# The scheduler counts a port of SBUF that VectorE and GpSimd take by turns; an expert's token rows are gathered two experts ahead

## The chip, the cores and the metric

The program runs on one core of a Trainium2 chip. What counts is the device time of one execution in microseconds (us), as the median of several runs. Five engines work side by side, each through its own queue in order: TensorE (PE, matmuls, with PEld for its weight loads), VectorE (DVE), ScalarE (ACT), GpSimd (POOL) and SyncE (SP, which here only issues DMAs and loads registers). An instruction waits on semaphores for others, and everything behind it in the same queue waits with it.

## What is computed

One encoder layer for 2048 tokens of width 1024: differential attention (4 heads with two score matrices each) beside gated linear attention (GLA), cross-attention to 256 memory tokens, and a mixture of 32 experts, of which each token takes two. The last part in the reference:

```python
def expert_block(args):
    xb, e = args
    hid = jax.nn.silu(xb @ w_gate[e]) * (xb @ w_up[e])
    return hid @ w_down[e]
```

and the differential attention, whose combination of two softmaxes is the place that most of the text below is about:

```python
p = probs(qb1, k1) - lam * probs(qb2, k2)
return jnp.einsum('bhqk,bhkv->bhqv', p.astype(v.dtype), v)
```

Matmuls run in float16 with each operand split into a high and a low half, three products for one. So every tensor that goes into a matmul is first split: ACT writes the high half, and DVE or POOL subtracts it from the float32 value to get the low half.

## The kernel before

Four stages follow each other. **Stage A1** (0 to about 625 us) projects the tokens and runs the GLA heads. **Stage A2** (to about 1155 us) is the differential attention, by blocks of 128 queries and 4 heads. **Stage C** (to about 1600 us) is the cross-attention and the routing of tokens to experts. **The MoE stage** runs the experts, two fixed ones first, then 30 that `rank` orders by their number of tokens.

In A2 each head goes twice (s = 0, 1) through a loop: `scores` has PE write up to four PSUM banks `sc` of 512 keys, DVE takes the minimum of each bank (`mx<-sc`) and of the four (`m<-mx`), ACT takes the exponential (`e<-sc,m`), which frees the banks for the next scores. Once both halves of a head are there, `combine` has DVE form `e1 + cc * e2` in float32 (`e<-e,cc`, a scalar_tensor_tensor with both operands in SBUF, in chunks of up to 1024 keys), ACT cast it (`e<-e`), POOL subtract the cast (`e<-e` on POOL), and SP transpose it by DMA (`pT<-e`) for PE's `po<-VC,pT`. `queries` has DVE copy and POOL subtract on a tile `qc`, `da_norm` and `out_proj` have DVE subtract on `mcd` and `hc`.

In the MoE stage `split_expert` loads an expert's weights in 12 DMAs of 0.5 MB (`est`, 8 buffers of tag E), which ACT and DVE split into `ew` (28 buffers of tag W, shared with the transposed tokens `exT`). `tokens` loads a list of row numbers (`lt<-lists`, issued by SP, with the expert's number read into a register by a TENSOR_LOAD of `order`), gathers the rows with an indirect DMA issued by POOL (`ex<-xnS,lt`, 4 buffers of tag Q), and has PE transpose them (`pxT`) and ACT and DVE copy them to `exT`. `expert` runs the matmuls `pgu` and `py`, and POOL issues the scatter-add `out_dram<-ey,lt`, which still reads `lt`, so a buffer of `lt` (6 of them) is free only after the scatter of its chunk. Each list, gather and scatter is for a chunk of up to 128 rows; most experts have two chunks.

The order on each engine is not written by hand. All operations are recorded, and `flush` runs a list scheduler over them: `price` gives each a cost in ns, `pick` takes for each engine the operation that could start first (ties within 1 ns go to the lower `prio`, which is the place in the program plus a shift by group and engine from the table `SHIFT`), and buffers are given out in the order of the program within a tag. A register load is priced at 100 ns. Before the change `pick` takes DVE and POOL as independent of each other:

```python
t = max(f, o.ready, lane[e][-8] + 110 if o.dma else 0)
```

The emitted order is fixed; on the chip only the waits move.

Of the kernel before, what the change touches and what calls it, by code (L numbers as in the profile page):

```python
# [8 lines left out]
F16 = mybir.dt.float16  # L9
# [29 lines left out]
THR = 0  # L39
# [15 lines left out]
        124, 122, 118, 118, 116, 114, 112, 112, 106, 104, 160, 176, 32]  # L55


TAGS = {"W": (4096, 28), "E": (4096, 8), "P": (4096, 3), "X": (4096, 4), "Q": (4096, 4), "t2": (2048, 4), "t1": (1024, 2), "r": (160, 5), "lt": (32, 6),
        "s8": (32, 5), "sq": (32, 6), "mx": (32, 8), "cb": (32, 6), "so": (32, 6), "c8": (32, 5), "c9": (32, 6), "q8": (32, 4), "grT": (512, 1)}
BANKS = {"mm": 3, "av": 1, "sc": 4}  # L60
AP = bass.AP
# [33 lines left out]

class Op:
    __slots__ = ("i", "eng", "method", "args", "kw", "cost", "need", "users", "ready", "prio", "opens", "tiles", "dma",
                 "start", "end", "fn", "group", "chain")


class Program:
# [4 lines left out]
    def __init__(self, nc, tc):  # L106
        self.nc, self.tc = nc, tc
        for e in ("tensor", "vector", "scalar", "gpsimd", "sync"):
            setattr(self, e, Engine(self, e))
        self.ops, self.tags, self.bufs = [], {}, {}  # L110
        self.log = {}
        self.shift, self.group = 0, ""
        self.chain = None
        self.free = {e: 0 for e in ("tensor", "vector", "scalar", "gpsimd", "sync")}
        self.dma_free = self.hw_free = 0
# [46 lines left out]
    def record(self, eng, method, a, k, fn=None):  # L162
# [48 lines left out]
        o.need = list(need)  # L211
        self.ops.append(o)
        return o

    @staticmethod
    def size(ap):
# [44 lines left out]
    def flush(self):  # L261
# [61 lines left out]
        while len(order) < n:  # L323
# [13 lines left out]
            if o.dma:  # L337
                if e == "gpsimd":
                    self.free[e] = t + 1040
                    s = t + 1770  # L340
                else:
                    self.free[e] = t + 60
                    h = max(self.hw_free, t + 120)
                    turn = "transpose" in o.method
                    s = max(self.dma_free, h + (1275 if turn else 1100))
                    self.hw_free = max(h + 1175, s + o.cost - 927) if turn else h + 475
                s = max(self.dma_free, s)
                self.dma_free = s + o.cost
# [39 lines left out]
class Layer:  # L388
# [1042 lines left out]
    def begin_moe(self):  # L1431

        nc = self.nc
        self.ident16 = self.gate_b[:, 128:192].bitcast(F16)
        nc.vector.tensor_copy(self.ident16, self.ident)
        which, need, self.first = self.expert_weights(None, 0)
        self.prog.shift = EARLY
        cap = CAPS[NE - FIXED]
        tokens = self.tokens(cap, which, need, blocks=LATE)
        self.second = self.expert_weights(None, 1, [self.last] if THR else [], CHAIN)  # L1440
        self.expert(cap, self.first, tokens)
        self.prog.shift = 0

    def stage_moe(self):
# [4 lines left out]
        ready = {}  # L1449

        def prepare(n):
            s = slots[n]
            if n == 0:
                which, need, w = lambda: NE, (), self.first
            elif n < FIXED:
                which, need, w = self.second
            else:
                if n == FIXED:
                    self.rank()
                which, need, w = self.expert_weights(s, None)  # L1460
            self.prog.shift = FRONT
            ready[n] = w, self.tokens(CAPS[s], which, need)
# [9 lines left out]
    def expert_weights(self, rank, e, after=(), chain=0):  # L1472

        nc, a, prog = self.nc, self.a, self.prog
        reg = []
        need = []
        if e is None:
            need = [prog.call("sync", lambda nc: reg.append(nc.sync.value_load(
                self.order[0:1, rank:rank + 1], min_val=0, max_val=NE - 1)), [], [self.order], method="value_load")]
        which = (lambda: reg[0]) if e is None else (lambda: e)  # L1480
        return which, need, self.split_expert(which, need + list(after), STAG if e == 0 else "E", chain)

    def split_expert(self, which, need, tag="E", chain=0):
        self.prog.group = "ew"
# [22 lines left out]
    def tokens(self, cap, which, need, first=None, blocks=0):  # L1507

        self.prog.group = "tk"
        nc, prog = self.nc, self.prog  # L1510
        xT = [self.tile("W", "exT", [8, cap], F16) for _ in range(2)]
        rest = []
        for t0 in range(0, cap, 128):
            n = min(128, cap - t0)
            lt = self.tile("lt", "lt", [2], I32)
# [2 lines left out]

            g = -(-n // 16) * 16
            m = g if parts == 1 else 128 // parts  # L1520
            rest.append((t0, m, lt, parts))

            def load(nc, lt=lt, m=m, t0=t0, parts=parts):
                e = which()
                if first is not None:
# [5 lines left out]
                if parts > 1:  # L1531
# [5 lines left out]
                out=x[:g].rearrange("p t d -> p (t d)"), out_offset=None, in_=self.xnS[:S + OFF - blocks * 128],  # L1537
                in_offset=bass.IndirectOffsetOnAxis(ap=lt[:g, 0:1], axis=0)), [x[:g]],
                      [lt[:g], self.xnS[:S + OFF - blocks * 128]])
            for h in range(2):  # L1540
                p = self.prog.tile(self.ps, [128, 8, 128], F16, "pxT", "mm", BANKS["mm"])
                for k in range(8):
# [65 lines left out]
    def stage_over(self):  # L1608
# [5 lines left out]
        with self.tc.For_i(0, total, 1):  # L1614
# [21 lines left out]
            self.expert(128, w, self.tokens(128, which, (), lambda: row))  # L1636


# [24 lines left out]
```

## Time and profile before

| | |
|---|---|
| median of 3 runs | 2382.82 us (2374.73 to 2393.74) |
| the profiled execution | 2377.83 us, span 2376.1 us |
| PE busy | 2137.9 us (90% of the span) |
| DVE busy | 1559.7 us (66%) |
| ACT busy | 1339.2 us (56%) |
| POOL busy | 750.6 us (32%) |
| mean DMA rate | 204 GB/s |

The profile is one execution, recorded by the hardware. Busy time is the time in which an engine had an instruction running; a wait is idle time of an engine, put down to what ended it. An instruction that the engine has started but that is held inside counts as busy, and shows only as a duration above that of its like. Rows of the profile name operations by the tiles they write and read, as `out<-in`.

### The profile page before, as it was taken

To read this page: it belongs to the slowest core of one execution; us is meant where nothing else is said; L and a number is where in the kernel's file an instruction comes from. 1 tells how busy PE (TensorE), PEld (TensorE's weight loads), DVE (VectorE), ACT (ScalarE), POOL (GpSimd) and SP (SyncE) were. 2 spreads that over 40 slices of the span, in tenths; PEclk is the share of its full clock that TensorE was granted. 3 is DMA by queue.
4 is the path that set the end of the run, shared out by engine and by line. 5 is a ranking of instruction groups with operands and counts; after the bars stand their busy time and mean duration, and the time that the engine had idled before them with its cause. 6 is when DMAs were issued, how large, how long until landed. Compare 5 with 4: busy or idle time off the path is not lost. (4 is left out here: it accounts for less than half of the span.)

```text
span 2376.1 us, 55935 instructions
## 1 busy us (share of the span) xinstructions
PE 2137.9 (90%) x22153; PEld 1466.6 (62%) x22153; DVE 1559.7 (66%) x3434; ACT 1339.2 (56%) x2848; POOL 750.6 (32%) x622
## 2 busy tenths in 40 slices
PE   6999999999888889889998999994899999888888
PEld 3456646556444445445665777843777887777666
DVE  7454445655588888888534655476666877777774
ACT  6455345554466666665433333444566777667775
POOL 1444235552134444444221222213132322222111
PEclk9999999999989999999999999997899999999999
DMA  9544246663357686888785556495989999999995
GB/s 258 155 114 116 81 142 178 192 191 103 111 116 149 145 179 151 184 169 201 168 211 131 116 143 126 117 250 140 300 303 329 345 369 331 325 338 340 358 346 152
DMA packets 504232, 485.34 MB, mean 204 GB/s; under 512 B 391364, under 2 KB 401886, under 8 KB 503966
## 3 DMA queue, kind: packets, MB, share of 16 engines
q1 hardware_dynamic: 489950, 442.11, 64.9%
q0 software_dynamic: 14016, 39.63, 7.2%
q8 instruction: 175, 2.87, 0.5%
q14 instruction: 91, 0.75, 0.1%
HBM read 306.28 MB, written 83.61 MB: 164 GB/s over the span
## 5 line engine op out<-in xcount | busy, mean ns | idle before, releaser
L166 DVE SCALAR_TENSOR_TENSOR ew<-est,ew 128x1024 f16<-128x1024 f32 x384 | 459.8, 1220 | 95.1 <-ACT ew L166 91.5
L166 PE MATMUL pgu<-exT,ew 128*128 128x160 f16 (+27 forms) x6336 | 451.5, 227 | 4.8 <-issue 2.3
L166 PEld LDWEIGHTS <-ew 128*128 128x128 f16 x6336 | 409.7, 100 | 13.6 <-issue 7.5
L166 ACT ACTIVATE ew<-est 128x1024 f16<-128x1024 f32 x384 | 392.8, 1051 | 33.7 <-DMA est<-in_w_e_down_dram 23.9
L166 PEld LDWEIGHTS <-uT 128*128 128x128 f16 x1920 | 187.7, 98 | 224.1 <-issue 9.7
L166 PE MATMUL py<-ew,hid 128*128 128x512 f16 (+4 forms) x1584 | 244.8, 348 | 8.2 <-DVE hid L166 6.2
L166 PE MATMUL sc<-KC,qT 128*128 128x512 f16 (+3 forms) x640 | 171.0, 359 | 57.9 <-ACT e L166 53.9
L166 ACT ACTIVATE e<-sc,m 128x512 f32<-128x512 f32 (+3 forms) x288 | 179.2, 631 | 75.6 <-DVE m L166 49.0
L166 POOL TENSOR_TENSOR e<-e 128x1024 f16<-128x1024 f32 (+7 forms) x96 | 152.3, 1591 | 215.5 <-ACT e L166 165.7
L166 DVE TENSOR_REDUCE mx<-sc 128x1 f32<-128x512 f32 (+3 forms) x320 | 185.4, 603 | 51.1 <-PE sc L166 50.8
L166 PE MATMUL ph<-wo,mT 128*128 128x512 f16 x768 | 194.2, 380 | 8.2 <-DMA mT<-mcd 3.9
L166 PE MATMUL pc<-hT,wcq 128*128 128x128 f16 x3072 | 193.8, 220 | 1.6 <-DMA hT<-hcS 1.0
L166 PEld LDWEIGHTS <-wcq 128*128 128x128 f16 x3072 | 181.6, 98 | 4.9 <-DMA hT<-hcS 1.5
L166 PE MATMUL phc<-wco,prT 128*128 128x512 f16 x768 | 175.9, 382 | 4.3 <-DMA prT<-prc 4.3
L166 PEld LDWEIGHTS <-hid 128*128 128x128 f16 (+4 forms) x1584 | 106.0, 104 | 108.9 <-issue 19.9
L1603 POOL DMA_INDIRECT out_dram<-ey,lt x33 | 65.0, 1969 | 263.9 <-ACT ey L166 218.2
L166 PEld LDWEIGHTS <-qT 128*128 128x128 f16 x640 | 60.0, 99 | 118.4 <-issue 75.8
L166 PE MATMUL po<-VC,pT 128*128 128x128 f16 x1632 | 123.1, 221 | 6.2 <-DMA pT<-e 4.9
L166 PEld LDWEIGHTS <-prT 128*128 128x128 f16 x768 | 74.2, 98 | 87.0 <-DMA prT<-prc 4.4
L166 PEld LDWEIGHTS <-mT 128*128 128x128 f16 x768 | 72.6, 98 | 83.2 <-DMA mT<-mcd 5.8
L166 PEld LDWEIGHTS <-pT 128*128 128x128 f16 x1632 | 103.6, 99 | 29.2 <-DMA pT<-e 9.7
L166 ACT CAST e<-e 128x1024 f16<-128x1024 f32 (+7 forms) x96 | 76.5, 798 | 69.1 <-DVE e L166 36.0
(320 smaller groups left out, 3700.1 us busy)
## 6 DMA issues: line engine op xcount, KB each, us to landing
est<-in_w_e_gate_dram SPq DMA_DIRECT2D x128, 512.0 KB
est<-in_w_e_up_dram SPq DMA_DIRECT2D x128, 512.0 KB
est<-in_w_e_down_dram SPq DMA_DIRECT2D x128, 512.0 KB
wst<-in_w_in_dram SPq DMA_DIRECT2D x20, 512.0 KB
xt<-in_x_dram SPq DMA_DIRECT2D x16, 512.0 KB
uS<-uT SPq DMA_DIRECT2D x16, 512.0 KB
ust<-in_w_ckv_dram SPq DMA_DIRECT2D x16, 512.0 KB
uT<-uS SPq DMA_DIRECT2D x16, 512.0 KB
```

The lines of the kernel that those rows point to most:

```text
L166: o.fn = fn or (lambda nc: getattr(getattr(nc, eng), method)(*a, **k))
L1603: self.prog.call("gpsimd", lambda nc: nc.gpsimd.indirect_dma_start(out=out, out_offset=bass.IndirectOffsetOnAxis(ap=rows, axis=0), in_=y, ...
```

## The change

`shares_port` marks the operations that use a port taken by turns: on GpSimd tensor_tensor and tensor_scalar with more than 8 columns, on VectorE two-input operations with both large operands in SBUF, and copies and tensor_scalar from SBUF to SBUF. In `flush` there is one more time, `port_free`: a marked operation can't start before it, on either engine, and sets it to its end. Costs, shifts and the operations themselves stay as they were, but the order on every engine is made anew with this rule.

In the MoE stage `tokens` is cut in two: `fetch` (the list and the gather) and `turn` (transposes and copies). `stage_moe` calls `fetch` for expert n+2 ahead of `turn` for expert n+1, and `lt` has 12 buffers instead of 6. `expert_weights` is cut likewise; the register load moves to `chosen`, which `fetch` calls.

```diff
-"t1": (1024, 2), "r": (160, 5), "lt": (32, 6),
+"t1": (1024, 2), "r": (160, 5), "lt": (32, 12),
...
+        o.port = self.shares_port(eng, method, outs, ins)
...
+    def shares_port(self, eng, method, outs, ins):
+
+        if eng == "gpsimd":
+            return method in ("tensor_tensor", "tensor_scalar") and self.size(outs[0]) > 8
+        n = sum(x.space != PSUM for x in ins)
+        if method in ("tensor_tensor", "scalar_tensor_tensor"):
+            return eng == "vector" and sum(x.space != PSUM for x in ins if self.size(x) > 1 or self.size(outs[0]) == 1) > 1
+        return eng == "vector" and method in ("tensor_copy", "tensor_scalar") and n > 0 and outs[0].space != PSUM
...
-                t = max(f, o.ready, lane[e][-8] + 110 if o.dma else 0)
+                t = max(f, o.ready, lane[e][-8] + 110 if o.dma else 0, self.port_free if o.port else 0)
...
                 self.free[e] = o.end = t + o.cost
+                if o.port:
+                    self.port_free = o.end
+                    dirty.update(("vector", "gpsimd"))
...
+        def prepare(n):
+            which, need, got = rows.pop(n)
+            w = self.first if n == 0 else self.second[2] if n < FIXED else self.split_expert(which, need)
+            self.prog.shift = FRONT
+            ready[n] = w, self.turn(CAPS[slots[n]], got)
+            self.prog.shift = 0
+        fetch(0)
+        fetch(1)
         prepare(0)
         for n, s in enumerate(slots):
+            if n + 2 < len(slots):
+                fetch(n + 2)
             if n + 1 < len(slots):
                 prepare(n + 1)
```

The first place is on DVE in stage A2, for one head of a block with 1792 keys: `mx` and `m1` are the minima that the loop waits for, `e_1367` and `e_1368` the two chunks of the head before. One piece of the difference:

```order
 L166 SCALAR_TENSOR_TENSOR cc_1406<-rs_1250,s2_1405,nlam_1019 128x1
-L166 SCALAR_TENSOR_TENSOR e_1367<-e_1379,cc_1406,e_1367 128x1024
 L166 TENSOR_REDUCE mx_1409<-sc_1410 128x1
 L166 TENSOR_REDUCE mx_1409<-sc_1411 128x1
 L166 TENSOR_REDUCE mx_1409<-sc_1412 128x1
 L166 TENSOR_REDUCE mx_1409<-sc_1413 128x1
+L166 TENSOR_SCALAR r1t_1285<-sst_1284 128x1
+L166 SCALAR_TENSOR_TENSOR e_1367<-e_1379,cc_1406,e_1367 128x1024
+L166 TENSOR_REDUCE m1_1414<-mx_1409 128x1
+L166 COPY r1_1143<-r1r_1286 128x1
 L166 SCALAR_TENSOR_TENSOR e_1368<-e_1380,cc_1406,e_1368 128x768
-L166 TENSOR_REDUCE m1_1414<-mx_1409 128x1
```

The first chunk moved behind the four minima, and both chunks now stand close together, with `m1` between them instead of behind the second.

The second place is on SP, where `rank` has just ordered the experts: `lt` are the lists of rows, TENSOR_LOAD reads an expert's number, `est` are the weights of the first ranked expert. The order before:

```order
L1533 DMA lt_3345<-lists_1034 128x1x2
L1478 TENSOR_LOAD order_3366
...
L1533 DMA lt_3401<-lists_1034 128x2
...
L1499 DMA est_3375<-in_w_e_gate_dram 128x1024
...
L1499 DMA est_3387<-in_w_e_up_dram 128x1024
L1478 TENSOR_LOAD order_3366
...
L1499 DMA est_3389<-in_w_e_up_dram 128x1024
```

The same place in the changed kernel:

```order
L1500 TENSOR_LOAD order_3348
...
L1556 DMA lt_3357<-lists_1034 128x2
...
L1556 DMA lt_3359<-lists_1034 96x2
...
L1556 DMA lt_3428<-lists_1034 128x2
...
L1525 DMA est_3383<-in_w_e_gate_dram 128x1024
...
L1525 DMA est_3387<-in_w_e_gate_dram 128x1024
L1500 TENSOR_LOAD order_3348
...
L1556 DMA lt_3475<-lists_1034 128x2
...
L1525 DMA est_3389<-in_w_e_gate_dram 128x1024
```

Before, one list and seven weight loads follow the first three register loads, and 20 register loads come ahead of the eighth weight load. Now five lists and three weight loads follow, and 26 register loads and two more lists come ahead of the fourth weight load.

The third place is on POOL a little later: `ex` with 96 rows is the second chunk of the second fixed expert, which PE waits for, and `ey` are the scatters of the experts ahead of it. The order before:

```order
L1536 DMA ex_3402<-xnS_1033,lt_3401 128x2048
L1603 DMA out_0_dram<-ey_3299,lt_3258 2176x1024
L1603 DMA out_0_dram<-ey_3302,dst_3304 8704x256
L1603 DMA out_0_dram<-ey_3358,dst_3360 8704x256
L1536 DMA ex_3406<-xnS_1033,lt_3405 96x2048
```

And in the changed kernel:

```order
L1559 DMA ex_3358<-xnS_1033,lt_3357 128x2048
L1637 DMA out_0_dram<-ey_3299,lt_3256 2176x1024
L1559 DMA ex_3360<-xnS_1033,lt_3359 96x2048
L1637 DMA out_0_dram<-ey_3302,dst_3304 8704x256
L1559 DMA ex_3380<-xnS_1033,lt_3379 128x2048
```

The gather of the 96 rows passed two scatters. Stage C keeps its order on every engine.

## Rows read from the trace of the kernel before

**Rows 1.** Windows by stage: length; busy PE, PEld, DVE, ACT, POOL; clock; DMA; GB/s

```profile
0.00:625.00 625.00, 578.48 (x5064) 350.80 (x5066) 326.98 (x757) 319.62 (x775) 244.51 (x181) 0.99 0.53 151
625.00:1155.00 530.00, 454.10 (x3355) 253.13 (x3352) 442.01 (x943) 335.73 (x856) 218.57 (x148) 0.97 0.74 159
1155.00:1600.00 445.00, 429.93 (x4910) 313.88 (x4909) 240.70 (x872) 163.75 (x426) 96.79 (x147) 0.99 0.64 156
...
1660.00:1760.00 100.00, 90.89 (x1118) 73.88 (x1117) 61.12 (x103) 60.53 (x93) 22.35 (x16) 0.90 0.91 293
1760.00:2340.00 580.00, 530.80 (x7068) 432.85 (x7067) 439.87 (x601) 423.06 (x636) 143.01 (x82) 0.96 1.01 342
```

**Rows 2.** Waits of 625 to 1155 us: who <- for whom: us in total, times, longest

```profile
ACT e L166 <- DVE m L166: 79.7, 48, 4.2
PE sc L166 <- ACT e L166: 53.9, 40, 5.6
DVE mx L166 <- PE sc L166: 50.8, 38, 4.5
```

**Rows 3.** Groups by form, DVE, 625 to 1155 us: count | busy us, mean ns | idle

```profile
L166 DVE SCALAR_TENSOR_TENSOR e<-e,cc 128x1024 f32<-128x1024 f32 x40 | 56.0, 1399 | 1.2
...
L166 DVE COPY qc<-qc 128x512 f16<-128x512 f16 x30 | 18.4, 618 | 1.9 <-POOL qc L166 1.0 <-ACT qc L166 0.7
...
L166 DVE SCALAR_TENSOR_TENSOR e<-e,cc 128x896 f32<-128x896 f32 x8 | 11.9, 1493 | 0.1
L166 DVE SCALAR_TENSOR_TENSOR e<-e,cc 128x768 f32<-128x768 f32 x8 | 11.9, 1491 | 0.2
L166 DVE SCALAR_TENSOR_TENSOR e<-e,cc 128x640 f32<-128x640 f32 x8 | 10.7, 1332 | 0.0
...
L166 DVE SCALAR_TENSOR_TENSOR e<-e,cc 128x384 f32<-128x384 f32 x8 | 8.2, 1024 | 0.1
L166 DVE SCALAR_TENSOR_TENSOR e<-e,cc 128x512 f32<-128x512 f32 x8 | 8.0, 1002 | 0.1
```

**Rows 4.** The same view for POOL, 625 to 1155 us

```profile
L166 POOL TENSOR_TENSOR e<-e 128x1024 f16<-128x1024 f32 x40 | 87.0, 2175 | 131.1 <-ACT e L166 109.9 <-issue 21.3
```

**Rows 5.** Timeline, 807 to 830 us: start, length, instruction [idle before, releaser]

```profile
807.10 1.01 POOL L166 TENSOR_TENSOR ror<-rot,mhalf 128x4 f32<-128x4 f32 x1 [3.15 <-DVE s L166]
807.64 1.28 DVE L166 SCALAR_TENSOR_TENSOR e<-e,cc 128x1024 f32<-128x1024 f32 x1
...
813.31 0.87 DVE L166 SCALAR_TENSOR_TENSOR e<-e,cc 128x640 f32<-128x640 f32 x1
...
823.63 1.28 DVE L166 TENSOR_REDUCE mx<-sc 128x1 f32<-128x512 f32 x2
...
824.72 2.13 POOL L166 TENSOR_TENSOR e<-e 128x1024 f16<-128x1024 f32 x1 [1.16 <-ACT e L166]
824.83 2.70 DVE L166 SCALAR_TENSOR_TENSOR e<-e,cc 128x640 f32<-128x640 f32 x1
...
828.25 0.28 DVE L166 COPY qc<-qc 128x512 f16<-128x512 f16 x1
828.45 0.14 DVE L166 TENSOR_REDUCE m<-mx 128x1 f32<-128x4 f32 x1
...
829.46 0.59 PE L166 MATMUL sc<-KC,qT 128*128 128x512 f16 x2 [1.71 <-ACT e L166]
```

**Rows 6.** MoE: register loads on SP, count: ns min/median/max, first and last start

```profile
L1478 SPq TENSOR_LOAD <-order x30: 261/268/815, 1655.0 to 1677.8; - x30
```

**Rows 7.** MoE, timeline of SP and of PE: lists, and a wait for gathered rows

```profile
1680.38 1.62 SPq L1533 DMA_DIRECT2D lt<-lists  x2
...
1694.05 0.82 PE L166 MATMUL pxT<-gb,ex 96*128 96x96 f16 x8 [4.78 <-DMA ex<-xnS,lt]
```

**Rows 8.** MoE, who waited for tile ex, and SP's waits: us, times, longest

```profile
  PE pxT L166: 20.7, 7
...
SPq L1533 <- DMA out_dram<-ey,lt: 35.4, 13, 6.0
```

More of the change, by code (lines that the diff above doesn't have):

```diff
@@ L55 @@
         124, 122, 118, 118, 116, 114, 112, 112, 106, 104, 160, 176, 32]
-TAGS = {"W": (4096, 28), "E": (4096, 8), "P": (4096, 3), "X": (4096, 4), "Q": (4096, 4), "t2": (2048, 4), "t1": (1024, 2), "r": (160, 5), "lt": (32, 6),
+TAGS = {"W": (4096, 28), "E": (4096, 8), "P": (4096, 3), "X": (4096, 4), "Q": (4096, 4), "t2": (2048, 4), "t1": (1024, 2), "r": (160, 5), "lt": (32, 12),
         "s8": (32, 5), "sq": (32, 6), "mx": (32, 8), "cb": (32, 6), "so": (32, 6), "c8": (32, 5), "c9": (32, 6), "q8": (32, 4), "grT": (512, 1)}
@@ L97 @@
     __slots__ = ("i", "eng", "method", "args", "kw", "cost", "need", "users", "ready", "prio", "opens", "tiles", "dma",
-                 "start", "end", "fn", "group", "chain")
+                 "start", "end", "fn", "group", "chain", "port")
 class Program:
@@ L114, in __init__ @@
         self.free = {e: 0 for e in ("tensor", "vector", "scalar", "gpsimd", "sync")}
-        self.dma_free = self.hw_free = 0
+        self.dma_free = self.hw_free = self.port_free = 0
     def tile(self, pool, shape, dtype, name, tag, bufs):
@@ L1435, in begin_moe @@
         nc.vector.tensor_copy(self.ident16, self.ident)
-        which, need, self.first = self.expert_weights(None, 0)
+        which, need, self.first = self.expert_weights(0)
         self.prog.shift = EARLY
         cap = CAPS[NE - FIXED]
-        tokens = self.tokens(cap, which, need, blocks=LATE)
-        self.second = self.expert_weights(None, 1, [self.last] if THR else [], CHAIN)
+        tokens = self.turn(cap, self.fetch(cap, which, need, blocks=LATE))
+        self.second = self.expert_weights(1, [self.last] if THR else [], CHAIN)
         self.expert(cap, self.first, tokens)
@@ L1448, in stage_moe, with fetch @@
         slots += [k + j * n for k in range(n) for j in range(3)]
-        ready = {}
-        def prepare(n):
+        ready, rows = {}, {}
+        def fetch(n):
             s = slots[n]
             if n == 0:
-                which, need, w = lambda: NE, (), self.first
+                which, need = lambda: NE, ()
             elif n < FIXED:
-                which, need, w = self.second
+                which, need, _ = self.second
             else:
@@ L1459, in prepare @@
                     self.rank()
-                which, need, w = self.expert_weights(s, None)
+                which, need = self.chosen(s)
             self.prog.shift = FRONT
-            ready[n] = w, self.tokens(CAPS[s], which, need)
+            rows[n] = which, need, self.fetch(CAPS[s], which, need)
             self.prog.shift = 0
+        def prepare(n):
[6 more added lines that the diff above has]
+        fetch(1)
         prepare(0)
         for n, s in enumerate(slots):
+            if n + 2 < len(slots):
+                fetch(n + 2)
             if n + 1 < len(slots):
@@ L1470, in stage_moe, with chosen, expert_weights @@
             self.prog.shift = 0
-    def expert_weights(self, rank, e, after=(), chain=0):
-        nc, a, prog = self.nc, self.a, self.prog
+    def chosen(self, rank):
         reg = []
[L1476 to L1481, printed above, removed]
+        need = [self.prog.call("sync", lambda nc: reg.append(nc.sync.value_load(
+            self.order[0:1, rank:rank + 1], min_val=0, max_val=NE - 1)), [], [self.order], method="value_load")]
+        return (lambda: reg[0]), need
+    def expert_weights(self, e, after=(), chain=0):
+        which = lambda: e
+        return which, [], self.split_expert(which, list(after), STAG if e == 0 else "E", chain)
     def split_expert(self, which, need, tag="E", chain=0):
@@ L1505, in split_expert, with fetch @@
         return get("w_e_gate", D, DE, 2), get("w_e_up", D, DE, 2), get("w_e_down", DE, D, 1)
-    def tokens(self, cap, which, need, first=None, blocks=0):
+    def fetch(self, cap, which, need, first=None, blocks=0):
         self.prog.group = "tk"
         nc, prog = self.nc, self.prog
-        xT = [self.tile("W", "exT", [8, cap], F16) for _ in range(2)]
-        rest = []
+        rows = []
         for t0 in range(0, cap, 128):
@@ L1520, in tokens @@
             m = g if parts == 1 else 128 // parts
-            rest.append((t0, m, lt, parts))
             def load(nc, lt=lt, m=m, t0=t0, parts=parts):
@@ L1539, in tokens, with turn @@
                       [lt[:g], self.xnS[:S + OFF - blocks * 128]])
+            rows.append((t0, n, x, m, lt, parts))
+        return rows
+    def turn(self, cap, rows):
+        self.prog.group = "tk"
+        nc = self.nc
+        xT = [self.tile("W", "exT", [8, cap], F16) for _ in range(2)]
+        rest = []
+        for t0, n, x, m, lt, parts in rows:
+            rest.append((t0, m, lt, parts))
             for h in range(2):
@@ L1635, in stage_over @@
             w = self.split_expert(which, ())
-            self.expert(128, w, self.tokens(128, which, (), lambda: row))
+            self.expert(128, w, self.turn(128, self.fetch(128, which, (), lambda: row)))
 def kernel(**inputs):
```

## The prediction

> **What bounds the kernel now.** I read the windows by stage first, because the change touches two stages in different ways. In A1 PE is busy for 578 of 625 us, in stage C for 430 of 445 us [rows 1]: both are PE's own work, and little can be won there by moving DVE or POOL. In A2 PE is busy for 454 of 530 us and DVE for 442 of 530 us, so neither is full and about 76 us of PE's time are idle. In the MoE stage from 1760 us the DMA engines are full (share 1.01, 342 GB/s) and PE is busy for 531 of 580 us: two limits lie close together there. Only in the 100 us after `rank` does DMA have some room (0.91, 293 GB/s) [rows 1].
>
> Then I read the waits in A2, to see what its idle 76 us are made of. They form one loop: PE waits for ACT's exponential (53.9 us in 40 waits), ACT waits for the minimum `m` (79.7 us in 48 waits), and DVE's `mx` waits for PE's scores (50.8 us) [rows 2]. Whatever delays `m` goes once around the loop and ends as idle PE. What delays `m` is not a wait that a view of waits could name. The timeline shows it as a duration: DVE needed 2.70 us for an `e` of 640 keys that took 0.87 us elsewhere, while POOL ran its own `e` of 1024 keys from 824.72 us for 2.13 us. `m` followed at 828.45 us, and PE's next scores at 829.46 us, after 1.71 us of idleness [rows 5].
>
> **Term 1, the combination in A2.** How much of DVE's time is such holding follows from the means by form. Clean prices from the timeline are 1.28 us for 1024 keys and 0.87 us for 640 [rows 5], so 0.41 us for 384 keys more; by that slope an `e` of 896, 768, 512 or 384 keys costs 1.14, 1.01, 0.73 or 0.60 us clean (estimates). Against the means [rows 3] the excess is 40 x 0.12 = 4.8 us for 1024 keys, then 8 x 0.35 = 2.8, 8 x 0.48 = 3.9, 8 x 0.46 = 3.7, 8 x 0.27 = 2.2 and 8 x 0.43 = 3.4 us for the shorter ones: 20.8 us together. The copies `qc` have a mean of 618 ns [rows 3] and took 0.28 us when POOL was idle [rows 5]: 30 x 0.34 = 10.1 us. Together DVE is held for about 31 us. That the shorter chunks suffer most fits the order: they stand directly behind the first chunk, when POOL works on what ACT has cast of it, and POOL takes 2.18 us for one of these [rows 4], 87.0 us in all.
>
> With the change the scheduler no longer plans a DVE `e` inside a POOL `e`. The order shows how it gets there: both chunks stand next to each other, ahead of POOL's work on the first, and the minima pass them. This removes no work; it only turns holding into useful order. Upper bound of the gain: all 31 us, which PE's 53.9 us of waiting for ACT [rows 2] could contain. Lower bound: 0, if the held instructions were those that nothing waited for, or if POOL is late instead and its `e` delays the transposes. On one hand the one example that I followed passed fully to PE (1.71 us of a holding of 2.70 - 0.87 = 1.83 us [rows 5]). On the other hand DVE is idle for 530 - 442 = 88 us in A2 [rows 1] and absorbs some holdings, and the planned times of the other engines are not those of the chip, so some collisions will come back at other places. I take half: **-15 us**.
>
> A row and a rule differ here. POOL's `ror` (4 columns) ran for 1.01 us from 807.10 us, and DVE's `e` that started inside it took 1.28 us, its clean time [rows 5]; so leaving ops of up to 8 columns unmarked costs nothing by the trace. The Trainium skill, page "SBUF — State Buffer", section "Who interferes with whom", says that whoever issues first gets the shared pair of ports for the whole instruction, and that the issue order, not the shape, decides who blocks. The long collisions agree with it; by its letter that `e` would have ended some 0.47 us later than it did, the small ops would go on holding DVE, and the gain would be nearer 10 than 15 us. The measurement decides, and the sum goes by the row.
>
> **Term 2, A1.** The same rule reorders pieces of A1, but PE has 578 of 625 us there [rows 1], and what is idle is spread over many short gaps. Bounds: a few us either way. I take 0; the work that hides it is PE's own, and if PE were late in the gated attention the cost would show as PE waits on DVE or POOL in A1.
>
> **Term 3, the gathers.** In the MoE stage PE waited 20.7 us in 7 waits for gathered rows [rows 8], once 4.78 us at 1694 us [rows 7], in the stretch in which DMA had room. SP waited 35.4 us in 13 waits for the scatter to free a list buffer [rows 8]; behind it in SP's queue stand the weight loads, which is why this can matter to PE too. Fetching two experts ahead with 12 list buffers should end most of both. But from 1760 us DMA is full [rows 1]; what PE doesn't wait for rows it will wait for weights, and SP's waits there cost nothing while enough loads are outstanding. So the bounds are 0 and -20.7 us (the SP waits lie within these, or are hidden by full queues), and I take the part in the stretch with room and a little more: -7 us.
>
> Against it stands what the change puts ahead of the first ranked expert's weights. Five lists stand before the first weight load instead of one: 4 more at 0.81 us (1.62 us for two [rows 7]) are 3.2 us. And 26 register loads with two more lists now come ahead of the fourth weight load, where before 20 came ahead of the eighth. 26 x 0.268 us [rows 6] and two lists are 8.6 us at least; by the pace of the 30 before, 22.8 us for all [rows 6], up to 20 us. Four weight loads of 0.5 MB, issued later than they were, are 2 MB, at 342 GB/s [rows 1] about 6 us of DMA work that isn't done in the meantime. Bounds 0 (the two fixed experts' matmuls cover it, and the weights are needed only behind these) and +9 us. I take +3, so term 3 is **-4 us**. The register loads lie in the same stretch as the wait of 4.78 us, so gain and loss will be seen side by side.
>
> **Sum.** -15 + 0 - 4 = -19 us. The profiled execution took 2377.83 us, so it would take about 2359; it lies 5 us below the median of the runs, 2382.82, from which the forecast is 2382.8 - 19 = **2364 us**.
>
> **Rivals.**
> *The holding only moves (nothing changes).* The plan's times are sums of priced costs, on the chip the engines drift by more than the 0.87 to 2.70 us that matter here, and POOL's `e` has 87.0 us [rows 4] that must lie somewhere beside DVE's 442 [rows 1]. For it: DVE and POOL are marked together for most of a block. Against it: the two chunks are now neighbours by order, which no drift undoes. The time would be 2382.8 - 4 = 2379 us.
> *More is won.* All 31 us of holding and most of PE's 20.7 us for rows go: 2382.8 - 31 - 17 = 2335 us. For it: the followed example passed on 94% of its holding. Against: full DMA in the MoE stage, idle DVE in A2.
> *Slower: the combination comes too late.* The `e` now stand behind four minima, 4 x 0.64 us = 2.6 us later [rows 5], and these minima themselves wait for PE's scores. Behind `e` stand ACT's cast, POOL's subtraction and the transposes, for which PE's `po` waits. Each of the 80 chunks of [rows 3] that makes PE wait that long costs 2.6 us; from one in seven on (11 x 2.6 = 29 us) it takes more than term 1 gives, and at one in five (16, so 42 us) the time is 2382.8 - 19 + 42 = 2406 us. For it: PE has no more than 76 us of room in A2 [rows 1]. Against: PE has the scores of the next heads to do meanwhile.
>
> **How the numbers follow.** The forecast has a chance of 0.48, and its own range is 2345 to 2380 us; the holding that only moves 0.22; more won 0.12; slower 0.18. The range has to leave out no more than 2 in 10: half of the large gain (0.06) falls below 2335 us, and most of the slower case (0.13) beyond 2400 us. 1% is about 24 us, and about what a measurement of this kernel can tell from no change, since its own runs spread from 2374.73 to 2393.74 us. Faster by over 1% (below 2359) are the large gain and some two fifths of the forecast, 0.12 + 0.20 = 0.32. Slower by over 1% (above 2407) is most of the slow case, 0.15. Within 1% is the rest, 0.53.
>
> **What the changed profile would show.** Right: the means of `e` on DVE fall towards 1.28 us (1024) and 0.87 us (640), `qc` towards 0.28 us; PE's wait for ACT's `e` in A2 falls from 53.9 us by about 15, and A2 becomes as much shorter; PE no longer waits for `ex`, SP's lists no longer wait for scatters. Wrong: these means fall and A2 keeps its length (then the held instructions were not on the path); POOL's `e` grows beyond 2.18 us by as much as DVE gains (the holding moved); PE waits for `pT` in A2 (the slower rival); or PE waits for the first ranked expert's weights around 1700 us for more than the 4.78 us that go (then the register loads cost what the gathers gave).

## The result and the profile after

The changed kernel took **2355.93 us** (median of 4 runs, 2353.85 to 2358.44), the kernel before 2380.76 us beside it (4 runs); the ratio is 0.989, with a 95% interval of 0.985 to 0.993. That is 25 us less, where 19 were forecast. The profiled execution of the changed kernel has a span of 2356.6 us (before 2376.1).

The sum is near, but its parts are not. To see that, one must not look at the stages by fixed times, since they shift, but ask when the same instruction starts in both traces:

| us from the start | before | after | moved |
|---|---|---|---|
| first `pq` (end of A1) | 578.2 | 577.9 | -0.3 |
| first `pc` (first matmul of stage C) | 1162.7 | 1146.6 | -16.0 |
| first `phc` (first output projection of stage C) | 1225.3 | 1225.1 | -0.1 |
| first `pgu` (first expert) | 1634.0 | 1637.6 | +3.6 |
| end of the last `py` | 2364.8 | 2345.5 | -19.3 |

A2 is 16 us shorter, all of that is gone 79 us later, and the time that is left at the end comes from the MoE stage alone: 730.8 us from the first `pgu` to the last `py` before, 707.9 us after.

The windows of the changed kernel, columns as in [rows 1]:

```profile
0.00:625.00 625.00, 581.66 (x5067) 353.13 (x5068) 331.17 (x758) 319.47 (x777) 239.72 (x181) 0.99 0.54 151
625.00:1155.00 530.00, 469.73 (x3509) 268.88 (x3509) 427.27 (x958) 338.18 (x861) 222.31 (x151) 0.95 0.75 166
1155.00:1600.00 445.00, 418.63 (x4712) 303.83 (x4710) 231.19 (x839) 158.15 (x415) 92.90 (x142) 0.98 0.59 145
...
1660.00:1760.00 100.00, 83.99 (x1064) 67.55 (x1065) 59.09 (x108) 54.40 (x87) 27.84 (x19) 0.90 0.91 299
1760.00:2340.00 580.00, 548.27 (x7432) 446.98 (x7430) 455.51 (x624) 438.62 (x663) 126.59 (x82) 0.97 0.99 342
```

In A2 PE did 154 matmuls more in the same 530 us, while DVE's busy time fell by 15 us. In the last window PE got through 364 matmuls more. (The last row's DMA rate still reads 342 GB/s, because its final weights landed before 2340 us here; a window that ends earlier is shown below.)

The waits of the same stretch of A2, in answer to [rows 2]:

```profile
DVE mx L166 <- PE sc L166: 55.1, 60, 3.0
ACT e L166 <- DVE m L166: 46.9, 34, 6.4
...
PE sc L166 <- ACT e L166: 26.6, 16, 2.6
```

PE's wait for the exponential fell from 53.9 to 26.6 us, ACT's wait for `m` from 79.7 to 46.9 us. And DVE by form, in answer to [rows 3]:

```profile
L166 DVE SCALAR_TENSOR_TENSOR e<-e,cc 128x1024 f32<-128x1024 f32 x40 | 51.5, 1287 | 0.8
L166 DVE COPY qc<-qc 128x512 f16<-128x512 f16 x30 | 17.4, 580 | 7.6 <-ACT qc L166 5.4 <-POOL qc L166 2.1
L166 DVE SCALAR_TENSOR_TENSOR e<-e,cc 128x896 f32<-128x896 f32 x8 | 11.0, 1374 | 0.1
L166 DVE SCALAR_TENSOR_TENSOR e<-e,cc 128x768 f32<-128x768 f32 x8 | 9.3, 1166 | 0.0
L166 DVE SCALAR_TENSOR_TENSOR e<-e,cc 128x640 f32<-128x640 f32 x8 | 7.9, 991 | 0.0
L166 DVE SCALAR_TENSOR_TENSOR e<-e,cc 128x512 f32<-128x512 f32 x8 | 5.9, 744 | 0.0
L166 DVE SCALAR_TENSOR_TENSOR e<-e,cc 128x384 f32<-128x384 f32 x8 | 5.9, 731 | 0.1
```

The 1024-key `e` is down to its clean price (1287 ns). The shorter forms are not, and `qc` is far from the 280 ns that the prediction hoped for: the copies hardly changed (618 to 580 ns). All six forms of `e` together lost 106.7 - 91.5 = 15.2 us, against 20.8 us that stood above the clean prices.

**Where the 16 us of A2 went.** The trace before and the trace after, cut at the first `pc` and the first `phc`:

```profile
0.00:1162.70 1162.70, 1039.27 (x8450) 607.07 (x8451) 772.57 (x1711) 657.18 (x1635) 464.65 (x331) 0.98 0.63 155
1162.70:1225.30 62.60, 62.34 (x802) 50.88 (x803) 24.38 (x71) 21.76 (x61) 10.45 (x17) 1.00 0.83 212
```

```profile
0.00:1146.60 1146.60, 1043.04 (x8425) 613.65 (x8425) 753.60 (x1702) 655.95 (x1634) 459.74 (x329) 0.97 0.63 157
1146.60:1225.10 78.50, 69.78 (x825) 55.28 (x826) 28.12 (x83) 22.22 (x61) 12.37 (x19) 0.93 0.67 173
...
1180.00:1190.00 10.00, 6.33 (x41) 3.59 (x40) 3.14 (x9) 1.72 (x4) 0.77 (x2) 0.98 0.47 120
1190.00:1200.00 10.00, 5.17 (x51) 4.68 (x51) 4.88 (x16) 5.00 (x14) 3.25 (x5) 0.50 0.49 131
```

Between the two marks PE had almost no idle time before (busy 62.34 of 62.60 us), but 8.7 us after; in the window from 1190 to 1200 us, in which it stood until 1192.47 us and then ran again, its granted clock was 0.50, that is, the lower of its two levels, 1.2 GHz. And 24 matmuls `ph` that were done ahead of the first `pc` now stand behind it (109 instead of 85, 25.9 us instead of 20.2). So of the 16 us about 6 were never won, only put off, and about 10 were won and lost again. PE's timeline shows where, after:

```profile
1192.47 0.35 PE L166 MATMUL pss<-ones,s2c 128*128 128x1 f16 x8 [6.14 <-DVE mf L166]
...
1193.13 1.12 PE L166 MATMUL po<-VC,pT 128*128 128x128 f16 x9 [0.31 <-DVE rct L166]
...
1195.99 0.50 PE L166 MATMUL po<-VC,pT 128*128 128x128 f16 x3 [1.74 <-DMA pT<-e]
1196.80 11.91 PE L166 MATMUL pc<-hT,wcq 128*128 128x128 f16 x184 [0.30 <-ACT ec L166]
```

And before:

```profile
1184.11 7.08 PE L166 MATMUL pc<-hT,wcq 128*128 128x128 f16 x124 [0.17 <-ACT e L166]
...
1191.03 0.34 PE L166 MATMUL pss<-ones,s2c 128*128 128x1 f16 x8
1191.23 3.51 PE L166 MATMUL pc<-hT,wcq 128*128 128x128 f16 x60
```

`pss` (the sums of squares that norm the cross-attention's queries) needs the one bank of PSUM (the memory that PE's matmuls write to) that `po` of the last blocks uses, and that is free only once DVE has formed `mf` from it. Before, 124 matmuls `pc` cover that time. After, nothing does: the whole of that `pc` (184 matmuls) stands behind `pss`. The chain of waits of the changed kernel runs through just this place:

```profile
1185.99 0.35 PE po L166 x6
...
1186.36 0.42 ACT sqo L166
...
1186.86 1.24 ACT hc L166 x3
...
1188.12 0.69 DVE hc L166
...
1190.40 1.03 POOL ror L166
```

From `po` the chain goes by a square on ACT, with ACT's and DVE's `hc` of another block in its way, and POOL's `ror` to `mf`: 6 us in which PE stood.

### The profile page after: what moved, and what is told of

It reads as the page before. It is cut to its first block, busy times and chain, and to the rows that moved or that the text cites. A ratio compares the mean times of both kernels' runs of the same rounds, so it can differ in the third digit from the quotient of the medians.

```text
span 2356.6 us, 55878 instructions
## 1 busy us (share of the span) xinstructions
PE 2141.2 (91%) x22153; PEld 1469.0 (62%) x22153; DVE 1545.7 (66%) x3434; ACT 1338.3 (57%) x2848; POOL 729.8 (31%) x622
## 4 chain that ended last, share of the span: by engine, by line
PE 38%; DMA 8%; DVE 4%; issue 4%; ACT 3%; POOL 2%; SPq 2%; another core or an unknown queue 0%; POOLq 0%; ACTq 0%; DVEq 0%
PE pgu L166 13%; PE py L166 8%; PE pc L166 5%; PE phc L166 4%; PE ph L166 2%; PE pcs L166 2%; ACT ew L166 1%; PE pxT L166 1%; DMA lists<-row,dest 1%; DMA est<-in_w_e_down_dram 1%; PE pq L166 1%; DMA xTr<-xc 1%; DVE ew L166 1%; DMA mT<-gS 1%; PE sc L166 1%
## 5 line engine op out<-in xcount | busy, mean ns | idle before, releaser
L166 PEld LDWEIGHTS <-ew 128*128 128x128 f16 x6336 | 404.7, 98 | 17.6 <-issue 11.6
L166 ACT ACTIVATE ew<-est 128x1024 f16<-128x1024 f32 x384 | 394.3, 1050 | 25.6 <-DMA est<-in_w_e_down_dram 14.9
L166 PE MATMUL ph<-wo,mT 128*128 128x512 f16 x768 | 199.0, 387 | 11.0 <-DMA mT<-gS 8.3
L166 PE MATMUL sc<-KC,qT 128*128 128x512 f16 (+3 forms) x640 | 172.2, 364 | 30.0 <-ACT e L166 26.6
L166 PE MATMUL po<-VC,pT 128*128 128x128 f16 x1632 | 133.7, 226 | 13.7 <-DMA pT<-e 10.0
L166 PEld LDWEIGHTS <-pT 128*128 128x128 f16 x1632 | 110.1, 102 | 39.5 <-DMA pT<-e 14.8
L1637 POOL DMA_INDIRECT out_dram<-ey,lt x33 | 56.6, 1714 | 237.1 <-ACT ey L166 211.9
L1559 POOL DMA_INDIRECT ex<-xnS,lt x52 | 65.0, 1250 | 173.2 <-PE pxT L166 144.9
L166 POOL TENSOR_TENSOR uhl<-ust,uhl 128x1024 f16<-128x1024 f32 x44 | 95.0, 2165 | 58.3 <-ACT uhl L166 54.2
```

The lines of the kernel that those rows point to most:

```text
L166: o.fn = fn or (lambda nc: getattr(getattr(nc, eng), method)(*a, **k))
L1559: prog.call("gpsimd", lambda nc, x=x, lt=lt, g=g: nc.gpsimd.indirect_dma_start(out=x[:g].rearrange("p t d -> p (t d)"), out_offset=None, i ...
L1637: self.prog.call("gpsimd", lambda nc: nc.gpsimd.indirect_dma_start(out=out, out_offset=bass.IndirectOffsetOnAxis(ap=rows, axis=0), in_=y, ...
```

## The experiments

Each run has its kernel before beside it on the same chip (2381.2 us for e1 to e4 and e9 to e11, 2386.3 us for e5 to e8); ratios are to that.

| run | what it is | median us | ratio [95%] | first `pc` | first `phc` | first `pgu` to last `py` |
|---|---|---|---|---|---|---|
| before | | 2380.8 | 1 | 1162.7 | 1225.3 | 730.8 |
| after | | 2355.9 | 0.989 [0.985, 0.993] | 1146.6 | 1225.1 | 707.9 |
| e1 | scheduler's rule alone | 2375.0 | 0.998 [0.995, 1.001] | 1143.0 | 1221.6 | 729.9 |
| e2 | fetch ahead, 12 lists | 2350.4 | 0.987 [0.983, 0.992] | 1157.6 | 1220.1 | 706.3 |
| e3 | 12 lists alone | 2358.5 | 0.990 [0.985, 0.994] | 1163.3 | 1225.9 | 710.7 |
| e4 | fetch ahead, 6 lists | 2378.1 | 0.999 [0.996, 1.001] | 1159.8 | 1222.4 | 728.1 |
| e5 | after, other order of `ph` | 2343.1 | 0.982 [0.978, 0.986] | 1147.6 | 1210.5 | 701.4 |
| e6 | after, rule for `e` alone | 2336.1 | 0.980 [0.976, 0.984] | 1141.5 | 1212.2 | 698.7 |
| e7 | before, POOL only writes `e` | 2353.0 | 0.984 [0.979, 0.990] | 1132.2 | 1194.6 | 741.4 |
| e8 | 8 lists alone | 2351.5 | 0.986 [0.982, 0.989] | 1162.5 | 1225.1 | 702.0 |
| e9 | before, e5's order of `ph` | 2395.0 | 1.006 [1.004, 1.008] | 1176.6 | 1239.4 | 732.1 |
| e10 | e6, other order of `ph` | 2333.6 | 0.981 [0.979, 0.983] | 1141.8 | 1204.2 | 706.2 |
| e11 | e10 with one ahead, 8 lists | 2327.0 | 0.979 [0.977, 0.981] | 1137.5 | 1199.9 | 701.8 |

The last three columns are read from one profiled execution each. Kernels with the same order up to stage C (before, e2, e3, e4, e8) differ by up to 6 us in the first `pc`, so a few microseconds there mean nothing. The distance from the first `pc` to the first `phc` is steadier: 62.4 to 62.9 us in ten of the traces, 78.5 and 78.6 us in the changed kernel and e1, 70.7 us in e6.

**e1 to e4: which half of the change, and which part of that half.** e1 is the kernel before with `shares_port` and `port_free` added. e2 is the changed kernel without them:

```diff
-        o.port = self.shares_port(eng, method, outs, ins)
+        o.port = False
```

> The kernel before with the scheduler's new rule alone; lists and gathers as before. Theory A (read off the two traces: in the changed kernel stage C's first matmuls began 16 us earlier, but its first output projection began at the same time as before, 1225 us): A2 is shorter by 15 to 20 us, all of it is lost again before 1230 us, and the total stays within 5 us of the kernel before, about 2381 us. Rival B (the prediction's sum): the A2 gain stays to the end, total 2366 us, 15 us less.

Theory A held: first `pc` 20 us earlier, first `phc` 4 us earlier, and 6 us less at the end (5 were allowed for), by a ratio that can't be told from no change (0.995 to 1.001). In e1 PE stands at the same `pss` for the same 6.14 us.

> The changed kernel without the scheduler's rule: lists and gathers two experts ahead, 12 list buffers. Theory A (the MoE stage of the changed trace was 23 us shorter): about 2358 us, with the whole gain behind 1650 us and PE waiting no more for gathered rows. Rival B (the prediction's sum): 4 us less than before, 2377 us.

2350.4 us, 8 us below theory A's 2358: the whole gain of the change, and rather more, comes with the fetch and its lists alone. PE has no wait for gathered rows left in this trace. The prediction's -4 us is out.

> The kernel before with 12 list buffers instead of 6 and nothing else; rows are fetched one expert ahead. Theory A1 (the gain in the MoE stage is SP's: it no longer stands still for scatters, 17 us in waits of over 0.5 us in the trace before): 15 to 20 us less than before, about 2363 us, with PE's waits for gathered rows mostly gone. Theory A2 (the gain is that rows come an expert earlier): within 4 us of before, about 2380 us, and PE still waits some 20 us for rows.

The edit of e3, a piece of one line:

```diff
-"r": (160, 5), "lt": (32, 6),
+"r": (160, 5), "lt": (32, 12),
```

> The fetch two experts ahead without the scheduler's rule and with the 6 list buffers of before, so the complement of the run with 12 lists alone. Theory A1: no gain, 2376 to 2385 us, since a list's buffer still comes free only with a scatter. Theory A2: 15 to 23 us less than before, about 2360 us.

These two are the clearest pair: one number alone gives 0.990, and all the rewriting of `tokens` without that number 0.999. (e3's 2358.5 us are some 5 us below theory A1's 2363.) In the traces, PE's waits for `ex` are gone with 12 lists, and 17.7 us in 6 waits with 6 lists (20.7 us in 7 before, [rows 8]). The stretch in which weights stream shows the same split. Before:

```profile
1760.00:2300.00 540.00, 495.99 (x6640) 405.35 (x6639) 409.86 (x563) 394.18 (x595) 139.71 (x80) 0.96 1.01 342
```

After:

```profile
1760.00:2300.00 540.00, 508.27 (x6816) 413.06 (x6814) 429.56 (x584) 413.45 (x620) 120.49 (x79) 0.97 1.02 354
```

e3 (12 lists alone), and e4 (fetch ahead with 6 lists):

```profile
1760.00:2300.00 540.00, 509.46 (x6802) 414.42 (x6800) 427.68 (x583) 411.43 (x618) 121.61 (x78) 0.97 1.02 354
```

```profile
1760.00:2300.00 540.00, 497.38 (x6654) 405.67 (x6653) 413.00 (x567) 397.34 (x599) 134.56 (x81) 0.97 1.01 342
```

So 342 GB/s was not the most that the DMA engines could do. With the waits for rows gone they moved 354 GB/s, 3.5% more; over 540 us that is 19 us of weights.

How one number does that is seen at one of the seven waits of the kernel before, at 1835 us:

```profile
1822.22 2.35 POOL L1603 DMA_INDIRECT out_dram<-ey,dst  x1 [9.64 <-ACT hid L166]
1824.87 1.91 POOL L1536 DMA_INDIRECT ex<-xnS,lt  x1 [0.30 <-issue]
1827.09 1.06 POOL L1536 DMA_INDIRECT ex<-xnS,lt  x1 [0.30 <-issue]
```

```profile
1835.62 0.54 PE L166 MATMUL pxT<-gb,ex 54*128 54x54 f16 x8 [4.56 <-DMA ex<-xnS,lt]
```

```profile
1830.00:1835.00 5.00, 1.06 (x20) 0.88 (x16) 4.22 (x5) 2.61 (x4) 2.00 (x1) 0.85 1.04 271
1835.00:1840.00 5.00, 4.38 (x47) 4.31 (x48) 0.00 (x0) 1.06 (x1) 0.00 (x0) 0.50 1.05 345
```

PE waits for the first of the two gathers: the DMA whose landing ends PE's wait was issued at 1824.87 us, right behind a scatter for which POOL had stood 9.64 us, and landed at 1835.58 us. With six lists the scheduler can place this gather no earlier, since a list comes free only with a scatter. PE stands for 4.56 us, then runs at the lower clock (0.50). As long as it stands it uses up no weights, so their buffers don't come free either: from 1830 to 1835 us the DMA engines moved 271 GB/s, though their share read 1.04. In e3, with 12 lists, the gather of the same rows stands ahead of that scatter and of two others:

```profile
1791.82 2.67 POOL L1536 DMA_INDIRECT ex<-xnS,lt  x1 [8.38 <-PE pxT L166]
1794.79 1.60 POOL L1603 DMA_INDIRECT out_dram<-ey,lt  x1 [0.30 <-issue]
```

PE uses these rows at 1837.32 us there, without a wait; in e8 below the gather went out at 1773.77 us and PE used the rows at 1821.15 us.

SP's own waits were not the cost. SP waited 35.4 us for scatters before [rows 8], 14.9 us after, 23.4 us in e3, and 41.3 us in e8 below, which is among the fastest. My theory A1 gave SP's stalls as the mechanism; the size came out near, but the mechanism is the place of the gather.

**e8: how many lists.** The edit, a piece of the same line:

```diff
-"r": (160, 5), "lt": (32, 6),
+"r": (160, 5), "lt": (32, 8),
```

> The kernel before with 8 list buffers (6 before, 12 in the change); rows one expert ahead. Theory A (what was short is room for one or two lists more, so that the list of the next expert no longer waits for the scatter of one that still computes): most of the gain of 12 lists is there with 8, 2357 to 2365 us, and PE no longer waits for rows. Rival: each buffer gives its share, and 8 give a third of it: 2372 to 2376 us.

```profile
1760.00:2300.00 540.00, 510.65 (x6773) 414.02 (x6774) 428.90 (x587) 410.01 (x619) 133.72 (x77) 0.97 1.02 357
```

Two lists more give all of it (2351.5 us, more than the 2357 to 2365 of theory A), and PE's waits for rows are gone: 6 lists are three experts of two chunks, and room for one expert more was enough.

**e5 and e9: the stall at the end of A2.** The table of shifts has a number for PE's output projections of the shorter blocks. It sets whether `ph` or `pc` goes first where both could; 1200 was taken because in the order that it makes `pss` stands between two pieces of `pc` again. The edit, a piece of one line:

```diff
-"OP:sync": 70, "OP:tensor": 904,
+"OP:sync": 70, "OP:tensor": 1200,
```

> The changed kernel with one number of the table of shifts altered (OP:tensor, PE's output projections of the blocks of up to 1024 keys, 904 to 1200), which gives PE another order at the end of A2, in which the wait for the scores of the last block no longer stands ahead of cross-attention matmuls that could run. Theory A (the A2 gain is lost in one stall of PE, 10 us of idle or half-clocked time at 1186 to 1197 us in the changed trace, that the order makes): PE has no gap there, phc starts some 8 to 12 us earlier than 1225 us, and the total is 2344 to 2348 us against 2356. Rival C (what comes before phc is bounded by something else, the loads of its weights or the chain of the last block): phc still starts at 1225 us within 3 us, total 2353 to 2358 us.

> A control for the run with OP:tensor 1200: the kernel before with that same number altered and nothing else. Theory A (1200 helped the changed kernel only because it took the stall out of the changed order; the kernel before has no such stall): no gain, 2378 to 2392 us. Rival (the number is better for any order): 2365 to 2374 us.

In e5 PE has no wait there, and `phc` comes 15 us earlier (8 to 12 were expected):

```profile
1176.47 0.34 PE L166 MATMUL pss<-ones,s2c 128*128 128x1 f16 x8
...
1210.47 4.26 PE L166 MATMUL phc<-wco,prT 128*128 128x512 f16 x19
```

From first `pc` to first `phc` it is 62.9 us, as before the change (62.6). The total fell to 2343 us, 13 us under the changed kernel. In the kernel before, the same number costs some 14 us (2395, ratio 1.006), a little more than I allowed for; what costs them is open. So the number isn't better in itself; it takes out a stall that the new order had made. Theory C, something fixed that bounds `phc`, is out.

**e7: is it POOL that holds DVE?** POOL's subtraction of `e` is replaced by an instruction that reads nothing; the scheduler is told the old price and the old operands, so that the order on PE, DVE and ACT stays that of the kernel before up to the MoE stage. The low halves of the probabilities are zero in this run.

```diff
-            nc.gpsimd.tensor_tensor(out=pc[:, w:2 * w], in0=e1, in1=pc[:, :w], op=OP.subtract)
+            self.prog.call("gpsimd", lambda nc, low=pc[:, w:2 * w]: nc.gpsimd.memset(low, 0.0),
+                           [pc[:, w:2 * w]], [e1, pc[:, :w]], method="tensor_tensor")
```

> The kernel before, its order on PE, DVE and ACT kept through stage C, with POOL's subtraction of e left out: POOL fills the low halves with zeros instead, an instruction that reads nothing and is shorter. Theory A (DVE's excess over its clean price is POOL's doing and delays PE's scores): DVE's e of 1024 keys falls to 1.28 us and the shorter ones to their clean prices, 1.07 ns per key; stage C's first matmul comes 15 to 25 us earlier than in the kernel before; the total is 2357 to 2367 us, since here no new order makes a stall. Rival D (the order with the minima ahead of e is what won in the changed kernel, not the holding): e falls, but stage C starts within 5 us of before, total 2376 to 2383 us.

```profile
L166 DVE SCALAR_TENSOR_TENSOR e<-e,cc 128x1024 f32<-128x1024 f32 x40 | 51.3, 1282 | 1.0
...
L166 DVE SCALAR_TENSOR_TENSOR e<-e,cc 128x640 f32<-128x640 f32 x8 | 7.0, 876 | 0.0
```

```profile
820.94 0.95 POOL L1053 MEMSET e<- 128x1024 f16 x1
821.31 0.87 DVE L166 SCALAR_TENSOR_TENSOR e<-e,cc 128x640 f32<-128x640 f32 x1
```

Every form of `e` is at its clean price, 876 ns for 640 keys where 1332 stood before. Stage C's first matmul starts 30 us earlier, more than any order gave, and this time `phc` does too (1194.6), since the order at the end of A2 is the old one. So in the old order the holding costs up to 30 us: the same order without it is that much faster. It is not quite a clean measure, because POOL's `e` is also shorter here (955 instead of 2175 ns), so the transposes start earlier. Nor does it tell what the new order won by, which is rival D's question; e6 below bears on that. The median is 2353.0 us, 4 us less than the 2357 to 2367 of theory A, with runs from 2341 to 2363 us, and in the profiled one the MoE stage took 10 us longer than before; why is open.

The second fence shows a short `e` on DVE beside a POOL fill, both at their own length. The Trainium skill, page "SBUF — State Buffer", section "Who interferes with whom", says that a DVE instruction with two inputs in SBUF contends with a GpSimd instruction that reads SBUF and not with one that only writes it; the row agrees: `e` took its clean 0.87 us, though it started inside a fill of 0.95 us.

**e6, e10, e11: a better version.** e6 marks only the combination in A2; e10 adds another number for `ph`; e11 is e10 with rows fetched one expert ahead, as before the change, and 8 lists.

```diff
-        o.port = self.shares_port(eng, method, outs, ins)
+        o.port = self.shares_port(eng, method, outs, ins) and self.group in ("c", "C")
...
-"OP:tensor": 904,
+"OP:tensor": 1000,
```

> The changed kernel with the scheduler's rule only for the combination in A2 (DVE's and POOL's operations on e), so that A1, queries and stage C are planned without it. Theory A (the gain in A2 comes from e alone): stage C's first matmul about 1145 us, as in the changed kernel and 17 us ahead of before; its end depends on the stall at the end of A2, of which this order has a smaller one: 2340 to 2352 us. Rival (the other marks matter too): first matmul of stage C at 1150 us or later, total as with the fetch alone, 2350 us or more.

> The kernel with the scheduler's rule for e alone and the fetch two experts ahead (2336 us), with OP:tensor 1000 instead of 904, whose order at the end of A2 has the wait for pss behind cross-attention matmuls. Theory A (what that kernel gave back after A2, 21 us ahead at stage C's first matmul and 13 at phc, was such a stall): 20 us ahead of the kernel before at both places, total 2327 to 2333 us. Rival (given back for another reason): 2334 to 2340 us.

> The same with 8 list buffers and the rows fetched one expert ahead, as in the kernel before, so that it differs from the run beside it only in the MoE stage. Theory A (list buffers are what counted, how far ahead the rows are fetched counts for nothing): within 4 us of the run beside it, 2325 to 2335 us. Rival (two experts ahead gives something of its own): 5 to 15 us slower than the run beside it.

e6 has stage C's first matmul 21 us ahead of before, so marking `e` alone gives all that the full rule gave in A2. Its 2336.1 us are 4 us below the range of theory A, and 20 us below the changed kernel. But it did not win by ending the holding. The stretch from the first `pq` to the first `pc`, before, after, in e6 and in e7, columns as in [rows 1]:

```profile
578.20:1162.70 584.50, 507.45 (x3862) 286.06 (x3861) 467.21 (x1023) 358.24 (x926) 226.55 (x157) 0.98 0.71 156
```

```profile
577.90:1146.60 568.70, 508.46 (x3836) 290.64 (x3835) 444.50 (x1014) 357.54 (x925) 226.42 (x155) 0.95 0.72 160
```

```profile
578.20:1141.50 563.30, 503.15 (x3858) 287.52 (x3858) 462.60 (x1021) 357.42 (x925) 225.40 (x157) 0.98 0.74 162
```

```profile
579.70:1132.20 552.50, 502.93 (x3861) 285.97 (x3859) 417.97 (x1023) 356.30 (x925) 142.49 (x157) 0.98 0.77 165
```

DVE's busy time, in which holding counts, fell by 22.7 us in the changed kernel and by 49.2 us in e7, but by only 4.6 us in e6: there the six forms of `e` lost 8.9 of their 106.7 us (those of 640 and 896 keys none), but other instructions were held more (`qc` 808 ns, 618 before). All the same ACT's wait for `m` fell from 79.7 to 55.6 us in e6, PE's wait for the exponential from 53.9 to 28.8 us, and the stretch became 21 us shorter. e10 and e11, with the same rule, agree (DVE 464.5 and 464.1 us, 565.0 and 562.4 us long). So an order can win as much with most of the holding left. That the minima passed `e`, as rival D has it, would fit, but no run changed that alone.

8 of e6's 21 us are lost again at the same place as in the changed kernel (PE waits 1.8 us at `pss`, then 1.7 us at `po`). e10 takes that out: 21 us ahead at both marks. But it ends only 2.5 us ahead of e6, just outside theory A's range, since 4 us are lost in stage C and 7 in the MoE stage; these sizes are those of the scatter between executions. e11 is the fastest, **2327.0 us, 2.1% under the kernel before** and 29 us under the changed one. One expert ahead with 8 lists was 6.6 us faster than two ahead with 12 (e10), which neither of its theories had. So two ahead isn't needed. Whether it gives something of its own is open: with 12 lists it was 8 us faster than the lists alone (e2 against e3), and in e11 the number of lists changed as well.

## Why the prediction came out as it did, point by point

**Term 1, mechanism: right about the holding, not shown for the gain.** DVE is held inside instructions by POOL's work on `e`, and that kept `m` late: without it A2 is up to 30 us shorter (e7). The new order took a part of the holding away. But that the gain in A2 came from this isn't shown, since e6 wins 21 us with DVE busy only 4.6 us less.

**Term 1, size in A2: right by luck.** I took half of 31 us, -15, and the first `pc` came 16 us earlier. But the 31 us was the wrong upper bound. I priced `e` and `qc` alone. Setting each DVE instruction of A2 in the trace before against the tenth percentile of its own form (excesses over 60 ns, summed) gives about 57 us, also on small ones such as `cc`; in the changed trace about 37 us are left, in e7 about 6 us, and in e6 about 54 us. The first `pc` came 16, 30 and 21 us earlier in these three, so the time won does not follow the holding removed, and a share of one half that passes to PE has nothing behind it.

**Term 1, "the gain stays to the end": wrong, and this is the step that failed first.** I read the order at one block of 1792 keys and wrote that stage C keeps its order. That is true of PE and POOL from the first `phc` on (DVE swaps a few instructions there), but not for the first cross-attention matmuls, which lie among A2's last blocks. There the new order put `pss` ahead of a `pc` that had covered its wait. About 6 us were work put off, about 10 us went into the stall and the lower clock behind it. None of the three rivals was this: the combination did not come too late, nor did the holding move to POOL (its 1024-key `e` takes 2183 ns, before 2175).

**Term 2, A1: right.** First `pq` 0.3 us apart.

**Term 3, the gathers: far too small.** -4 forecast, -23 us measured from first `pgu` to last `py` (e2 -24.5, e3 -20, e8 -29). The step that failed: "from 1760 us DMA is full; what PE doesn't wait for rows it will wait for weights". A share of 1.01 was read as a ceiling; without PE's stalls it was 1.02 at 354 GB/s, and in e8 357. The stalls went and the rate rose; in one of them it was down to 271 GB/s, at a share of 1.04. That a PE that stands uses up no weights explains this, but is argued and not measured by itself. So the whole of the 20.7 us [rows 8] counted, and more: behind four of the seven stalls the granted clock was 0.53 to 0.71 in the next 5 us, too. The bound of -20.7 us stood in the text; I took the wrong end of it, and the measured gain reaches or passes even that.

**Term 3, the loss: seen.** Three of the first ranked expert's weight loads went out at 1664.9 us, the fourth only at 1685.0 us:

```profile
1664.91 1.51 SPq L1525 DMA_DIRECT2D est<-in_w_e_gate_dram  x3
1685.00 0.22 SPq L1525 DMA_DIRECT2D est<-in_w_e_gate_dram  x1
```

That is the upper bound of 20 us for the register loads. PE's busy time from 1660 to 1760 us is 84.0 us, where it was 90.9 us [rows 1]; 3.6 us of that is the later start of this stage. In the 100 us behind the first `pgu` PE is busy for 84.4 us before and 80.7 us after; in e3 and e2, also with 12 lists, for 80.2 and 82.8 us, and with 8 lists (e8) for 85.6 us. So +3 is about right, and by these runs it comes with the 12 lists.

**SP's waits for list buffers: right to count them at nothing, wrong to expect them to end.** 14.9 us of them are left in the changed kernel, and e8 keeps 41.3 us.

So -15 and -4 were forecast; in the two profiled executions -16 + 16 and -23 happened, with 4 us lost in stage C, -19 in all. The total came out near the forecast because two errors of like size stood against each other: that the total was near is luck.

**The range.** Its 2345 to 2380 us were said to leave out 0.19, but only what falls below 2335 and beyond 2400 us was counted. By the prediction's own times the large gain (2335) lies outside the range and the holding that only moves (2379) at its edge, so it left out more than 2 in 10.

## What to carry to other kernels

When an engine stands for a late transfer and its inputs stream through a ring of buffers, a DMA share of 1.0 is no proof of a bound: look at whether the stalls themselves throttle the stream, and at what the gather stands behind in its queue. When a scheduler's order is made anew, compare not one typical place but each seam between stages, and compare traces by when the same instruction starts. A gain that shows at one mark and not at the next has been lost between them, and the wait in that stretch names the pair of instructions to swap. A duration above that of its like shows that an engine is held; whether a new order wins by ending that is seen only when its busy time between the same two marks is compared too.

## What the runs showed of the hardware

- A POOL instruction that only writes SBUF did not lengthen DVE's two-input `e` (a mean of 876 ns for 640 keys); one that reads it did (1332 ns before).
- In the windows of 5 and 10 us in which PE took up work again after standing 4.56 and 6.14 us, its granted clock was 0.50 (1835 us before, 1190 us after), so these stalls cost more than their own length.
- The DMA share as shown goes above 1, and 1.01 at 342 GB/s left 3.5 to 4.4% to be had (354 and 357 GB/s); in a stall it read 1.04 at 271 GB/s.
